# A two-layer streaming encoder on one core: grouping the up projections' high and low products, taking gate rows and two modulation folds from rounded halves, and moving the score mask from TensorE to VectorE

## The chip, the cores and the metric

The kernel runs on one core of one Trainium2 chip. The metric is the device time of one execution in microseconds (us), the median of several runs. The engines are called as the profile calls them: PE (TensorE's matmuls), PEld (its weight loads), DVE (VectorE), ACT (ScalarE), POOL (GpSimd) and SP (SyncE, which issues nearly all transfers).

## What is computed

Two layers with 256 positions, width 2048 and batch 1. Each layer first derives six modulation vectors from the conditioning vector `c`, then runs a mixer over four head groups and a gated feed-forward network:

```
mod = (silu(c) @ w_mod[l] + b_mod[l]).reshape(bn, 6, d)
h = layer_norm(x) * (1.0 + scale_m) + shift_m
proj = h @ w_in[l]                       # 2048 -> 4288, split among four groups
...
y = jnp.concatenate([y_a, y_b, y_c, y_d], axis=-1) @ w_out[l]
x = layer_norm(ALPHA * x + (1.0 + gate_m) * y, post_mix_g[l], post_mix_b[l])
h = layer_norm(x) * (1.0 + scale_f) + shift_f
y = conv_ffn(h, w_up[l], w_conv[l], b_conv[l], w_down[l])   # 2048 -> 2 x 5632 -> 2048
x = layer_norm(ALPHA * x + (1.0 + gate_f) * y, post_ffn_g[l], post_ffn_b[l])
```

Group B is an attention with four heads: within a block of 128 queries the first 64 may not see the last 64 keys (the mask is by chunks of 64). Everything is float32.

## The kernel before, in words

**Products from halves.** A float32 product costs PE two matmul records with the full operands. Where the kernel can, it instead splits a float32 operand into a rounded high half of type float32r and a low half (the rest), and sums three products: high x high, high x low and low x high. For the weights ACT writes the high half (`act.copy`, line 403) and DVE the low one (`tensor_tensor` subtract, line 404); for activations `split` (lines 418 to 421) does the same. The high and low weight tiles, `whi` and `wlo`, each hold 1024 columns and come from the pool `splitp` with four buffers for each name. The raw weights lie in four buffers of 8 KB per partition (`rawp`), which the modulation's weights (`wmod`) and the weights of the projections (`wraw`) share.

**One unit.** `stream` (lines 347 to 355) is the basic step. It issues the load and the split of the next unit's weights, then the products of the unit before (`flush`), and then `pump` advances the modulation stream by as many steps as the stage's rate in `RATES` allows. So a unit's weights are prepared while PE works on the unit before it. The framework's scheduler then orders each engine's instructions; an engine executes its own in that order, and waits where a result is not there yet.

**Up projections.** `group2` (lines 474 to 497) computes 512 channels of the up projection for all 256 positions, in four units of four 128-row weight tiles. It keeps four PSUM accumulators of 128 channels by 512 columns: columns 0 to 255 collect the products with the high half of the activations and columns 256 to 511 those with the low half. For each weight tile and each accumulator it issues one matmul with the high weights and 512 columns (line 491) and right behind it one with the low weights and 256 columns (line 492). There are 40 such groups: 9 for gates (`g_c`) and 10 for values (`v_c`) in layer 0, and 10 and 11 in layer 1. The down projection (`out_proj`, accumulators `d`) and the output projection (`o`) use 512 columns throughout; the mixer's `group` uses 256 columns throughout.

**Modulation.** `mod_stream` (lines 265 to 310) loads `w_mod` row tile by row tile and DVE accumulates it, scaled by `c`, into `macc`, [128 x 2048] (`mod_step`, line 211). What is left is the sum over the 128 partitions. For shifts and scales `mod_cols` (lines 190 to 204) makes columns: one float32 matmul for each 128 columns of `macc`, with `macc` as the weights and a column of ones as the moving operand. For gates `gate_rows` (lines 244 to 252) makes a row in all partitions: four float32 matmuls with a [128 x 128] tile of ones as weights and 512 columns of `macc` moving. `settle` (lines 258 to 263) calls one or the other, two steps into the next vector at the latest or when the result is needed.

**Attention.** `mix_b` (lines 870 to 1036) computes scores for four heads into `ps_sc`. For each head and query block there are two score products (lines 986 and 987) and a third matmul with one row of weights (line 988, `ind_row` and `neg_row`, both rows of the constant `cst`) that adds -1e30 where the mask forbids. DVE then takes the row maxima (line 991), ACT the exponentials, DVE the scaling, PE the transposes. The scheduler places products of the mixer's next group C (`C_c`) between these steps on PE. In layer 0 group C uses unsplit float32 weights (`wexact`, line 379), which lie in the same `whi` and `wlo` buffers as the halves.

**Start.** `ones` is set by POOL (lines 100 and 101); ACT computes silu of `c` (line 118), whose result the first modulation step needs.

Of the kernel before, what the change touches and what calls it, by code (L numbers as in the profile page):

```python
# [7 lines left out]
F32 = mybir.dt.float32  # L8
# [46 lines left out]
def encoder_kernel(ctx: ExitStack, tc: tile.TileContext, A: dict, consts: bass.AP, out: bass.AP):  # L55
# [44 lines left out]
    ones = keep.tile([P, P], F32, name="ones")  # L100
    pool.memset(ones, 1.0)
# [6 lines left out]
    ind_row = cst[64:65, 256:384]  # L108
    neg_row = cst[64:65, 384:448]
# [95 lines left out]

    def mod_step(acc, w, kt, first):
        col = cact[:, kt : kt + 1]
        if first:
            i = dve.tensor_scalar(out=acc, in0=w, scalar1=col, scalar2=None, op0=ALU.mult)
# [264 lines left out]
    def group2(w, c0, name, then, bg=0, spare=0):  # L474
# [5 lines left out]
        def products(item, u):  # L480
# [248 lines left out]
    def mixers(l, w_in, Y, hF=None, between=None):  # L729
# [140 lines left out]
        def mix_b(cps, _):  # L870
# [106 lines left out]
            for blk in range(2):  # L977
                nkey = P * (blk + 1)
                per = 512 // nkey
                for g in range(4 // per):  # L980
                    ps = ms_tile("ps_sc")
                    for i in range(per):
# [8 lines left out]
                    dve.tensor_reduce(out=sm[:, 0:per], in_=p3, axis=AX.X, op=ALU.max)  # L991
# [409 lines left out]
def _constants():  # L1401
# [18 lines left out]
    c[64, 256:320] = 1.0  # L1420
    c[64, 384:448] = NEG
# [32 lines left out]
```

## Time and profile before

| | |
|---|---|
| median of 3 runs | 2338.86 us (2335.3 to 2343.4) |
| the profiled execution's own time | 2342.81 us |
| its span in the profile | 2341.0 us |
| mean granted clock of PE | 0.986 |
| instructions on DVE, ACT, POOL | 2241, 1429, 59 |
| transferred | 605.19 MB, mean 259 GB/s |

The layer 0 mixer runs to about 334 us, its output projection to 438, its up projections to 974, its down projection to 1224; layer 1's mixer ends at 1476, its output projection at 1569, its up projections at 2085, its down projection at 2329. In the profile each matmul of the float32 kind shows as two records. The busy time of a matmul is modelled from its start to the end of its pipeline, so neighbours overlap; the distance from one start to the next is what it costs PE.

### The profile page before, as it was taken

The page shows a single profiled execution, that of the slowest core. Times are in us where ns is not written, and L with a number is a line of the kernel's source. Part 1 is how long each engine was busy: PE and PEld are TensorE (multiplying, and loading weights), DVE is VectorE, ACT ScalarE, POOL GpSimd, SP SyncE. Part 2 cuts the span into 40 slices and gives each one's busy share as a digit, 9 for nine tenths or more (in the row PEclk, how much of TensorE's full clock was granted, in tenths as well). Part 3 has the DMA queues.
Part 4 walks back from the last instruction along what each step waited for, and adds up shares of the span by engine and source line. Part 5 has one row for each costly group of instructions (what it writes and reads, how often), then busy time and mean ns, then how long its engine had stood idle before and what let it go on. Part 6 is the DMA issues. An engine that isn't in the chain of part 4 may idle for free. (4 is left out here: it accounts for less than half of the span.)

```text
span 2341.0 us, 31348 instructions
## 1 busy us (share of the span) xinstructions
PE 2273.2 (97%) x12407; PEld 1940.7 (83%) x12407; DVE 1784.2 (76%) x2241; ACT 1012.0 (43%) x1429; POOL 36.0 (2%) x59
## 2 busy tenths in 40 slices
PE   6899999999999999999999999989999999999997
PEld 4688886698888888888879999869888888888786
DVE  6868987778888788889975798886777755665676
ACT  2221141245445444544544434435454454454553
POOL 2000000000000000000000000000000000000000
PEclk9999999999999999999999999999999999999999
DMA  9999889588888798898865576774767655555554
GB/s 338 367 318 333 283 274 383 202 304 288 311 311 302 280 333 314 279 351 306 313 212 173 173 242 211 271 274 165 254 229 262 224 180 194 184 185 194 180 197 144
DMA packets 228731, 605.19 MB, mean 259 GB/s; under 512 B 14676, under 2 KB 27204, under 8 KB 210916
## 3 DMA queue, kind: packets, MB, share of 16 engines
q1 hardware_dynamic: 227800, 602.30, 73.7%
q8 instruction: 97, 1.59, 0.3%
q0 software_dynamic: 784, 0.90, 0.1%
q14 instruction: 50, 0.41, 0.1%
HBM read 601.05 MB, written 2.10 MB: 258 GB/s over the span
## 5 line engine op out<-in xcount | busy, mean ns | idle before, releaser
L404 DVE TENSOR_TENSOR wlo<-wraw,whi 128x1024 fp32r<-128x1024 f32 (+1 forms) x622 | 748.0, 1215 | 352.2 <-ACT whi L403 344.6
L403 ACT CAST whi<-wraw 128x1024 fp32r<-128x1024 f32 (+1 forms) x622 | 645.8, 1045 | 759.9 <-PE g_c L83 224.3
L83 PE MATMUL v_c<-hT,whi 128*128 128x512 f32 (+1 forms) x1456 | 499.3, 391 | 0.0
L83 PE MATMUL g_c<-hT,whi 128*128 128x512 f32 (+1 forms) x1344 | 452.4, 387 | 0.0
L83 PE MATMUL v_c<-hT,wlo 128*128 128x256 f32 x1400 | 395.2, 282 | 0.0
L83 PE MATMUL d<-whi,a 128*128 128x512 f32 x1344 | 389.4, 391 | 0.0
L211 DVE SCALAR_TENSOR_TENSOR macc<-wmod,cact,macc 128x2048 f32<-128x2048 f32 (+2 forms) x180 | 358.4, 1991 | 37.6 <-DMA wmod<-in_w_mod_dram 36.4
L83 PE MATMUL g_c<-hT,wlo 128*128 128x256 f32 x1280 | 359.5, 281 | 0.0
L83 PEld LDWEIGHTS v_c<-hT,whi 128*128 128x128 f32 x1456 | 271.6, 189 | 62.8 <-ACT whi L403 0.2
L83 PEld LDWEIGHTS d<-whi,a 128*128 128x128 f32 x1344 | 253.7, 189 | 53.2 <-issue 0.5
L83 PEld LDWEIGHTS g_c<-hT,whi 128*128 128x128 f32 x1344 | 248.3, 188 | 56.0
L83 PEld LDWEIGHTS v_c<-hT,wlo 128*128 128x128 f32 x1400 | 266.3, 190 | 0.4 <-DVE wlo L404 0.2
L83 PEld LDWEIGHTS g_c<-hT,wlo 128*128 128x128 f32 x1280 | 242.0, 189 | 0.0
L83 PE MATMUL d<-wlo,a 128*128 128x512 f32 x672 | 234.8, 392 | 0.7 <-DVE wlo L404 0.7
L83 PEld LDWEIGHTS d<-wlo,a 128*128 128x128 f32 x672 | 126.9, 189 | 27.9 <-DVE wlo L404 1.2
L420 ACT CAST a<-g 128x512 fp32r<-128x512 f32 x132 | 81.4, 617 | 63.1 <-PE d L83 62.1
L83 PE MATMUL o<-whi,a 128*128 128x512 f32 x352 | 99.8, 391 | 0.2 <-ACT whi L403 0.2
L756 DVE SCALAR_TENSOR_TENSOR convD<-gluD,pm,convD 128x255 f32<-128x255 f32 (+26 forms) x240 | 98.8, 459 | 0.5
L421 DVE TENSOR_TENSOR a<-g,a 128x512 fp32r<-128x512 f32 x132 | 88.7, 685 | 10.4 <-ACT a L420 10.3
L83 PE MATMUL D_c<-hT,whi 128*128 128x256 f32 x432 | 84.2, 296 | 2.7 <-ACT hT L420 2.0
L1210 DVE SCALAR_TENSOR_TENSOR u<-g,pf,u 128x254 f32<-128x254 f32 (+1 forms) x176 | 74.3, 477 | 10.7 <-ACT u L86 10.7
L211 DVE SCALAR_TENSOR_TENSOR qacc<-wmod,cact,qacc 128x1024 f32<-128x1024 f32 (+1 forms) x75 | 80.3, 1070 | 2.6 <-DMA wmod<-in_w_mod_dram 0.5
(297 smaller groups left out, 2514.2 us busy)
## 6 DMA issues: line engine op xcount, KB each, us to landing
wraw<-in_ffn_w_up_dram SPq DMA_DIRECT2D x168, 1024.0 KB, 5.7
wmod<-in_w_mod_dram SPq DMA_DIRECT2D x136, 1024.0 KB, 6.1
wraw<-in_ffn_w_down_dram SPq DMA_DIRECT2D x88, 1024.0 KB, 5.3
wmod<-in_w_mod_dram SPq DMA_DIRECT2D x64, 512.0 KB, 9.0
wraw<-in_w_in_dram SPq DMA_DIRECT2D x30, 1024.0 KB, 5.5
wexact<-in_w_in_dram SPq DMA_DIRECT2D x52, 512.0 KB, 7.3
wmod<-in_w_mod_dram SPq DMA_DIRECT2D x32, 768.0 KB, 6.3
wraw<-in_w_out_dram SPq DMA_DIRECT2D x24, 1024.0 KB, 7.1
```

The lines of the kernel that those rows point to most:

```text
L83: pe.matmul(o, lhsT, rhs, start=start, stop=stop, skip_group_check=True)
L211: i = dve.scalar_tensor_tensor(out=acc, in0=w, scalar=col, in1=acc, op0=ALU.mult, op1=ALU.add)
L403: act.copy(hi[:, :m], r)
L404: i = dve.tensor_tensor(out=lo[:, :m], in0=r, in1=hi[:, :m].bitcast(F32), op=ALU.subtract)
L420: act.copy(hi, src)
L421: dve.tensor_tensor(out=lo, in0=src, in1=hi.bitcast(F32), op=ALU.subtract)
L756: dve.scalar_tensor_tensor(out=yd[:, j, 30 - k :], in0=glu[:, j, : S - 30 + k], scalar=CW(k, j), in1=yd[:, j, 30 - k :], op0=ALU.mult, op1 ...
L1210: dve.scalar_tensor_tensor(out=u[:, sh:], in0=x[:, : S - sh], scalar=col(k, j), in1=u[:, sh:], op0=ALU.mult, op1=ALU.add)
```

## The change

There are four edits.

1. `group2`: for each pair of accumulators all high products of the unit's four weight tiles come first (eight matmuls of 512 columns), then all low ones (eight of 256 columns).
2. `gate_rows`: `macc` is split into float32r halves by ACT and DVE (new function `halves`, with its tiles in the `whi` and `wlo` buffers of `splitp`), and for each 512 columns two float32r matmuls with float32r ones as weights replace one float32 matmul.
3. `mod_rows` (new) replaces `mod_cols` for layer 1's feed-forward shift and scale only: the halves are summed by eight float32r matmuls of 512 columns whose weights are four columns of zeros and ones, so that row j of a [4 x 512] result is the j-th quarter; ACT copies it, four PE transposes turn it to columns, and DVE adds the bias.
4. The mask: the sixteen one-row matmuls go, and before each row maximum DVE adds -1e30 to 64 partitions of the scores in PSUM.

Besides, `ones` is now part of a float32r tile `onesR`, which POOL fills in pieces in a temporary and ACT copies.

```diff
+    flat = tmp_tile("flat")
+    pool.memset(flat[:, 0:P], 1.0)
+    pool.memset(flat[:, P : P + 16], 0.0)
+    for j in range(4):
+        pool.memset(flat[:, P + 5 * j : P + 5 * j + 1], 1.0)
+    onesR = keep.tile([P, P + 16], F32R, name="onesR")
+    act.copy(onesR, flat[:, : P + 16])
+    ones = onesR[:, 0:P].bitcast(F32)
...
+    def halves(acc, c0):
+        hi = splitp.tile([P, 1024], F32R, tag="whi", name="mhi")
+        lo = splitp.tile([P, 1024], F32R, tag="wlo", name="mlo")
+        split((hi, lo), acc[:, c0 : c0 + 1024])
+        return [(hi[:, i * 512 : (i + 1) * 512], lo[:, i * 512 : (i + 1) * 512]) for i in range(2)]
+
+    def mod_rows(l, m, acc):
+        ps = ms_tile("ps_row")
+        for j, pair in enumerate(halves(acc, 0) + halves(acc, 1024)):
+            for n, part in enumerate(pair):
+                mm(ps[0:4, :], onesR[:, P + 4 * j : P + 4 * j + 4], part, j + n == 0, j + n == 4)
+        row = tmp_tile("mrow")
+        act.copy(row[0:4, :], ps[0:4, :])
+        ps = ms_tile("ps_mod")
+        for i in range(4):
+            pe.transpose(ps[:, 4 * i : 4 * i + 4], row[0:4, i * P : (i + 1) * P], ident[0:4, 0:4])
+        cols = keep.tile([P, KT], F32, name=f"mod_{l}_{m}")
+        done = dve.scalar_tensor_tensor(
...
     def gate_rows(l, m, acc):
-        for q in range(4):
-            c = slice(q * 512, (q + 1) * 512)
-            ps = ms_tile("ps_gate")
-            mm(ps, ones, acc[:, c], True, True)
-            ident_act(g[:, c], ps, 1.0, ones[:, 0:1])
+        for h in range(2):
+            for i, (hi, lo) in enumerate(halves(acc, h * 1024)):
+                c0 = h * 1024 + i * 512
+                ps = ms_tile("ps_gate")
+                mm(ps, onesR[:, 0:P], hi, True, False)
+                mm(ps, onesR[:, 0:P], lo, False, True)
+                ident_act(g[:, c0 : c0 + 512], ps, 1.0, ones[:, 0:1])
...
+        elif (l, m) in ((1, SHIFT_F), (1, SCALE_F)):
+            mod_rows(l, m, acc)
...
             for part in (range(0, 2), range(2, 4)):
-                for k, (hi, lo) in enumerate(item):
-                    kt = u * nk + k
-                    both = box["h"][kt // 2][2][:, kt % 2, :, :]
-                    for i in part:
-                        o = box["c"][i]
-                        off = slice(i * P, (i + 1) * P)
-                        mm(o, hi[:, off], both.rearrange("p h t -> p (h t)"), kt == 0, False)
-                        mm(o[:, :S], lo[:, off], both[:, 0, :], False, kt == KT - 1)
+                for i in part:
+                    for k, (hi, _) in enumerate(item):
+                        kt = u * nk + k
+                        both = box["h"][kt // 2][2][:, kt % 2, :, :].rearrange("p h t -> p (h t)")
+                        mm(box["c"][i], hi[:, i * P : (i + 1) * P], both, kt == 0, False)
+                for i in part:
+                    for k, (_, lo) in enumerate(item):
+                        kt = u * nk + k
+                        high = box["h"][kt // 2][0][:, kt % 2, :]
+                        mm(box["c"][i][:, :S], lo[:, i * P : (i + 1) * P], high, False, kt == KT - 1)
...
-                        mm(o, rope[:, h // 2, qs], rope[:, 2 + h % 2, :nkey], False, False)
-                        mm(o[:, nkey - 64 :], ind_row, neg_row, False, True)
+                        mm(o, rope[:, h // 2, qs], rope[:, 2 + h % 2, :nkey], False, True)
                     sm = smallp.tile([P, 16], F32, tag="sm", name="sm", bufs=3)
                     p3 = ps.rearrange("p (i k) -> p i k", i=per)
+                    ahead = p3[0:64, :, nkey - 64 :]
+                    dve.tensor_scalar(out=ahead, in0=ahead, scalar1=NEG, scalar2=None, op0=ALU.add)
                     dve.tensor_reduce(out=sm[:, 0:per], in_=p3, axis=AX.X, op=ALU.max)
```

How the scheduler places this is read from the order of instructions on an engine. On PE, in layer 0's up projections, the first fold of layer 1 (the shift, `ps_mod`) stands between two groups before the change; `g_c` and `v_c` are the accumulators of the gate group that ends there and the value group that begins, `whi` and `wlo` the halves of the weights, `hT` the activations:

```order
L83 MATMUL g_c_5772<-hT,whi 128x512
L83 MATMUL g_c_5772<-hT,wlo 128x256
L83 MATMUL g_c_5773<-hT,whi 128x512
L83 MATMUL g_c_5773<-hT,wlo 128x256
L83 MATMUL ps_mod<-bcol_98,cst 128x16
L83 MATMUL ps_mod<-ones,macc 128x1 x16
L83 MATMUL v_c_5993<-hT,whi 128x512
L83 MATMUL v_c_5993<-hT,wlo 128x256
L83 MATMUL v_c_5994<-hT,whi 128x512
L83 MATMUL v_c_5994<-hT,wlo 128x256
```

The same place on PE after the change (`mhi` and `mlo` are the halves of `macc`, `ps_row` the [4 x 512] sum):

```order
L83 MATMUL g_c_5798<-hT,wlo 128x256 x4
L83 MATMUL g_c_5799<-hT,wlo 128x256 x4
L83 MATMUL ps_row<-mhi,onesR 4x512
L83 MATMUL v_c_6025<-hT,whi 128x512 x4
L83 MATMUL ps_row<-mlo,onesR 4x512
L83 MATMUL ps_row<-mhi,onesR 4x512
L83 MATMUL ps_row<-mlo,onesR 4x512
L83 MATMUL ps_row<-mhi,onesR 4x512
L83 MATMUL v_c_6026<-hT,whi 128x512 x4
L83 MATMUL v_c_6025<-hT,wlo 128x256
L83 MATMUL ps_row<-mlo,onesR 4x512
L83 MATMUL ps_row<-mhi,onesR 4x512
```

High and low products now stand in runs of four to one accumulator, and the fold's matmuls stand among the next group's products.

The second place is SP's order at the end of layer 0's mixer. `wexact` are group C's weights (a unit of C takes two), `wmod` those of the modulation, `wraw` those of the output projection that follows. Before:

```order
L381 DMA wexact<-in_w_in_dram 128x1024 x2
L299 DMA wmod<-in_w_mod_dram 128x1536 x2
L381 DMA wexact<-in_w_in_dram 128x1024 x2
L299 DMA wmod<-in_w_mod_dram 128x1536 x3
L381 DMA wexact<-in_w_in_dram 128x1024 x2
L389 DMA wraw<-in_w_out_dram 128x2x1024
L299 DMA wmod<-in_w_mod_dram 128x1536 x2
L389 DMA wraw<-in_w_out_dram 128x2x1024
```

After:

```order
L420 DMA wexact<-in_w_in_dram 128x1024 x2
L338 DMA wmod<-in_w_mod_dram 128x1536 x5
L428 DMA wraw<-in_w_out_dram 128x2x1024
L338 DMA wmod<-in_w_mod_dram 128x1536 x2
L428 DMA wraw<-in_w_out_dram 128x2x1024
L420 DMA wexact<-in_w_in_dram 128x1024 x4
L338 DMA wmod<-in_w_mod_dram 128x1536 x2
L428 DMA wraw<-in_w_out_dram 128x2x1024
```

The weights of C's last two units moved behind modulation tiles and the first two tiles of the output projection. In the program the halves of the first gate, which take buffers of the same names, now stand ahead of them.

On ACT the program's first instructions are now a table load, the copy to `onesR`, another table load and then silu of `c`; before there were one table load and silu.

More of the change, by code (lines that the diff above doesn't have):

```diff
@@ L99, in encoder_kernel @@
     sinT = cst[:, 768:1024]
-    ones = keep.tile([P, P], F32, name="ones")
-    pool.memset(ones, 1.0)
+    flat = tmp_tile("flat")
[6 more added lines that the diff above has]
+    ones = onesR[:, 0:P].bitcast(F32)
     mhalf = keep.tile([P, 4], F32, name="mhalf")
@@ L106, in power @@
         pool.tensor_tensor(out=o, in0=i, in1=mhalf[:, : i.shape[1]], op=ALU.pow)
-    ind_row = cst[64:65, 256:384]
-    neg_row = cst[64:65, 384:448]
     X = []
@@ L204, in mod_cols @@
             MOD_BY[(l, m, k0 + j)] = done.ins.name
+    def halves(acc, c0):
[15 more added lines that the diff above has]
+        done = dve.scalar_tensor_tensor(
+            out=cols.rearrange("p (i j) -> p i j", i=4),
+            in0=ps[:, 0:KT].rearrange("p (i j) -> p i j", i=4),
+            scalar=0.0 if m == SHIFT_F else 1.0,
+            in1=bcol[l][:, m * KT : (m + 1) * KT].rearrange("p (j i) -> p i j", i=4),
+            op0=ALU.add,
+            op1=ALU.add,
+        )
+        for k in range(KT):
+            at = 4 * (k % 4) + k // 4
+            MOD[(l, m, k)] = cols[:, at : at + 1]
+            MOD_BY[(l, m, k)] = done.ins.name
     def mod_step(acc, w, kt, first):
```

2 lines of the change are left out of this document (removed).

## The prediction

> **What bounds the kernel now.** I read the page first, for the busy shares and the clock over the span.
>
> ```profile
> PE 2273.2 (97%) x12407; PEld 1940.7 (83%) x12407; DVE 1784.2 (76%) x2241; ACT 1012.0 (43%) x1429; POOL 36.0 (2%) x59
> PE   6899999999999999999999999989999999999997
> DMA  9999889588888798898865576774767655555554
> ```
>
> PE works throughout; the transfers are dense only in layer 0, the first half. Then I read the chain that ended last, and the waits.
>
> ```profile
> by line: PE g_c L83 11.0%; PE v_c L83 10.6%; PE d L83 9.4%; DMA wraw<-in_ffn_w_down_dram 0.5%; DVE x L658 0.2%; PE ps_xT L533 0.2%; DVE x L655 0.2%; PE ps_gate L83 0.2%; issue 0.1%; DVE wlo L404 0.1%; DVE st_o1q L664 0.1%; ACT whi L403 0.1%
> ...
> 1583.12 0.44 PE ps_xT L533 x4
> ...
> 1610.75 22.61 PE v_c L83 x128
> ...
> 2085.62 119.75 PE d L83 x528
> ```
>
> ```profile
> DVE wlo L404 <- ACT whi L403: 344.6, 269, 4.4
> ...
> ACT whi L403 <- PE g_c L83: 224.3, 138, 3.5
> ```
>
> The chain is PE without a break, one group of 128 matmuls every 22.61 us. ACT waits for PE to release a weight buffer, not the reverse, so the feeders are ahead. The windows of an up stretch in each layer say by how much:
>
> ```profile
> 540.00:660.00 120.00, 120.00 (x682) 104.02 (x681) 102.45 (x108) 57.63 (x79) 0.00 (x0) 1.00 0.87 307
> 1700.00:2080.00 380.00, 380.00 (x2153) 329.54 (x2152) 247.17 (x318) 193.66 (x279) 0.00 (x0) 1.00 0.62 209
> ```
>
> DVE is busy 85% of the time in layer 0 and 65% in layer 1. What shortens PE's stream therefore shortens the kernel, with less reserve in layer 0.
>
> **Grouping the up products.** A pair (512 columns high, 256 low) costs 22.61/64 = 353.3 ns in the chain. Runs of 512 columns alone, in the down projection above, cost 119.75/528 = 226.8 ns each. For 256 columns alone I take the mixer's group C in the timeline:
>
> ```profile
> 1401.57 0.40 PE L83 MATMUL C_c<-hT,whi 128*128 128x256 f32 x2
> ...
> 1405.53 0.40 PE L83 MATMUL C_c<-hT,whi 128*128 128x256 f32 x2
> ```
>
> Between these starts lie 33 matmuls of 256 columns, 3.96/33 = 120 ns each. Two pure runs thus cost 226.8 + 120 = 346.8 ns a pair, 6.5 less than alternating. That alternation does not always pay this shows in one stretch, where it ran at the pure rate. From the first row of a group to that of the next:
>
> ```profile
> 833.24 0.39 PE L83 MATMUL g_c<-hT,whi 128*128 128x512 f32 x1
> ...
> 855.43 0.39 PE L83 MATMUL v_c<-hT,whi 128*128 128x512 f32 x1
> ```
>
> That is 22.19/64 = 346.7 ns. The pairs are counted in the groups by form:
>
> ```profile
> L83 PE MATMUL v_c<-hT,whi 128*128 128x512 f32 x1344 | 478.8, 400 | 0.0
> L83 PE MATMUL g_c<-hT,whi 128*128 128x512 f32 x1216 | 429.2, 397 | 0.0
> ```
>
> Of 2560 pairs five groups (320, from 833 to 944 us) ran fast already; 2240 x 6.6 ns = 14.8 us are to be had. A switch from high to low and back is left once in eight pairs, which keeps between 0 and 1.9 us of that. I take -13.9 us.
>
> The page "TensorE: Matmul & The Clock Gate" of the Trainium skill gives, under "Back-to-back issue gap", N/2.4 + 2.5 ns from start to start of an isolated matmul, thus 325 ns for a pair in either order, and no gain from grouping; the rows show 353 and 347, so here the trace differs from it.
>
> **The two folds.** Before, each is a run of small matmuls between two groups. The timeline at both places, and the windows of the clock behind them (the column before the DMA share):
>
> ```profile
> 805.69 0.29 PE L83 MATMUL ps_mod<-bcol,cst 128*128 128x16 f32 x2
> ...
> 809.40 0.48 PE L83 MATMUL v_c<-hT,whi 128*128 128x512 f32 x1
> ```
>
> ```profile
> 944.17 0.29 PE L83 MATMUL ps_mod<-bcol,cst 128*128 128x16 f32 x2
> 944.31 5.01 PE L83 MATMUL ps_mod<-ones,macc 128*128 128x1 f32 x32
> 949.19 0.77 PE L83 MATMUL v_c<-hT,whi 128*128 128x512 f32 x1
> ```
>
> ```profile
> 810.00:813.00 3.00, 3.00 (x11) 2.51 (x11) 2.72 (x5) 2.79 (x6) 0.00 (x0) 0.50 0.00 0
> 947.00:953.00 6.00, 6.00 (x23) 5.42 (x24) 2.85 (x4) 3.32 (x7) 0.00 (x0) 0.50 0.30 126
> ```
>
> The folds take 3.71 and 5.02 us, and during or after them the granted clock is 0.50, which costs the next group half of 3.0 us and half of 3.8 (949.19 to 953): 1.5 and 1.9. Together 12.1 us. After: eight matmuls of 512 columns at 227 ns and four transposes (0.44 us in the chain above for larger ones), 2.3 us each, 4.5 in all, spread among full-size products. That is -7.6 us if the clock stays up, -4.2 if it still drops; I take -7, near the first, because no drop is seen among full-size products here.
>
> **The gates.** The first of four:
>
> ```profile
> 306.01 3.78 PE L83 MATMUL ps_gate<-macc,ones 128*128 128x512 f32 x8
> 309.63 0.59 PE L83 MATMUL C_c<-hF,wexact 128*128 128x256 f32 x2
> ```
>
> It holds PE for 3.62 us; after, eight products of 227 ns, 1.82. Four times 1.8, less a little since part of the 3.62 is waiting: -6.8 us.
>
> **What the halves cost.** Six steps (four gates, two folds) copy and subtract twice each. From the page:
>
> ```profile
> L404 DVE TENSOR_TENSOR wlo<-wraw,whi 128x1024 fp32r<-128x1024 f32 (+1 forms) x622 | 748.0, 1215 | 352.2 <-ACT whi L403 344.6
> L403 ACT CAST whi<-wraw 128x1024 fp32r<-128x1024 f32 (+1 forms) x622 | 645.8, 1045 | 759.9 <-PE g_c L83 224.3 <-PE v_c L83 172.9 <-PE d L83 134.8
> ```
>
> That is 12 x 1.05 us on ACT and 12 x 1.22 on DVE. The work itself fits into their idle time. But each step takes two of the four buffers of `whi` and `wlo`, so the unit after next can be split only when PE releases the unit before it, not a unit earlier. Its first copy (1.05) and subtraction (1.22) begin about a quarter of a unit (1.4 us) before PE needs them; its second ones begin at the unit's end. In the up stage the low halves are wanted only after eight high products (1.8 us), so about 0.5 us is left uncovered; in the output and down projections, which are not regrouped, about 0.7 to 1. Behind these subtractions DVE holds the modulation steps, which nothing waits for at once. I take +4 us for the six, between 0 and 10.
>
> In layer 0's mixer the order on SP moves the weights of C's last two units back until C's fourth-last and third-last units have released their buffers.
>
> ```profile
> wexact<-in_w_in_dram SPq DMA_DIRECT2D x52, 512.0 KB, 7.3
> ```
>
> ```profile
> 312.65 10.96 PE L83 MATMUL C_c<-hF,wexact 128*128 128x256 f32 x50
> ```
>
> They land 7.3 us after issue; a C unit of 16 products is 32 records, at 10.96 us for 50 about 7 us. Issue at the end of one unit thus meets the start of the next but one narrowly: +1 us, between 0 and 3.
>
> **The mask.** On PE its cost is from its start to the next product's:
>
> ```profile
> 1395.47 0.43 PE L83 MATMUL ps_sc<-cst 1*128 1x64 f32 x2
> 1395.84 0.49 PE L83 MATMUL ps_sc<-kn,qn 128*128 128x128 f32 x2
> ```
>
> 0.37 us, sixteen times: -5.9 us. On DVE six additions in PSUM come in. The trace has none; the nearest rows are the maximum over the same tile and a four-element operation:
>
> ```profile
> 1399.25 0.68 DVE L991 TENSOR_REDUCE sm<-ps_sc 128x4 f32<-128x512 f32 x1
> ...
> 1400.22 0.22 DVE L992 TENSOR_SCALAR sm<-sm,rr 128x4 f32<-128x4 f32 x1
> ```
>
> Between 0.22 and 0.68, about 0.4 for half the size, 2.4 in all on the score chain. PE has products of C to do meanwhile, and the scheduler has put the transposes further behind; I charge +1 (0 to 4).
>
> **The start.** ACT has a copy and a second table load ahead of silu, and POOL five more small fills.
>
> ```profile
> 0.73 1.28 ACT L118 ACT_TABLE_LOAD   x1 [0.73 <-PEq L1433]
> 3.02 0.31 ACT L118 ACTIVATE crow<-crow 16x128 f32<-16x128 f32 x1 [1.01 <-DMA crow<-in_c_dram]
> ```
>
> ```profile
> 14.33 0.49 DVE L209 TENSOR_SCALAR qacc<-wmod,cact 128x512 f32<-128x512 f32 x1 [0.29 <-DMA wmod<-in_w_mod_dram]
> ```
>
> Silu moves from 3.0 to about 4.5 us; its first user starts at 14.33. Cost nothing, as long as that transfer ends last.
>
> **The sum.** -13.9 - 7 - 6.8 + 4 + 1 - 5.9 + 1 = -27.6 us. The profiled execution took 2342.81 us (1.8 of it outside the span), which gives 2315.2; I forecast **2315 us**. It is the slowest but one of what was shown: the median of the runs is 2338.86, 4 us less, against which the forecast is 24 us or 1.0% faster. I do not carry those 4 us over: runs of before can differ in how many groups fall into the fast alternation, and grouped runs have no such choice.
>
> **The rivals.**
>
> - *The order of high and low does not matter.* What costs 6.6 ns a pair is then not the switch but something that runs of eight have too. For it: the stretch at 833 us switches and pays nothing. Against it: pure runs never show more than 227 and 120 ns. The first term falls away: 2315 + 14 = 2329 us. The Trainium skill's formula above would have it so.
> - *The halves break the feeding.* Each of the six steps leaves PE idle for the copy and subtraction of a whole unit, twice 1.05 + 1.22 = 4.5 us instead of 0.7: 6 x 3.8 = 23 us more, 2338 us, no change. For it: DVE at 85% in layer 0. Against it: the scheduler has put the low products of the gates behind the next group's high ones.
> - *Slower: the low tiles are held longer.* With all low products last, a unit's first `wlo` buffer is read until 0.24 us before the unit's end instead of 1.4; the next subtraction in that buffer, and with it the raw buffer and the next transfer, come 1.17 us later. It decides once DVE has no idle time left in a unit. In layer 0's 76 units (19 groups of 4), half of them late by 1.17 us give +44: 2359 us. Against it: the 15% idle there, and that low products are wanted 1.6 us later too.
>
> **How the numbers follow.** The forecast gets 0.76, the first rival 0.1, the second 0.1, the third 0.04. The forecast's own bounds: every gain full and no stall is 14.8 + 7.6 + 7.2 + 5.9 = 35.5, 2307 us; stalls of 10, C late by 3, the mask's 4 and the clock still dropping (2.8) give 2315 + 14 = 2329, where the first rival lies as well. So 2306 to 2329, with the second and third rival left out. About 0.3% (7 us) is what a measurement can tell from no change: faster by more, under 2331.8, is forecast and first rival and part of the second, 0.9; the same 0.06; slower 0.04.
>
> **What would show it.** In the profile of the changed kernel a group of 128 up matmuls should take 22.2 us throughout; the clock should be 1.00 around the two folds; the gates' eight products should each be 227 ns apart; 16 one-row matmuls should be gone. PE waiting for `wlo` after a gate or fold, or for `wexact` before the end of C, shows the charges. Groups still at 22.6 us, or PE waiting for `wlo` in every layer 0 unit, make the prediction wrong.

## The result and the profile after

| | before | after |
|---|---|---|
| median, same chips | 2337.55 us (2330.69 to 2345.99, 10 runs) | 2329.73 us (2323.61 to 2334.77, 10 runs) |
| the profiled execution | 2342.81 us | 2328.31 us |

The ratio is 0.9962, with a 95% interval of 0.9945 to 0.9978: faster by 7.8 us or 0.4%. The forecast was 2315 us with a range of 2306 to 2329, so the time lies 0.7 us above the range and the gain is about a third of what was forecast against the median.

The page of the kernel after shows PE busy 97% as before, of a shorter span:

```profile
PE 2255.9 (97%) x12331; PEld 1936.7 (83%) x12331; DVE 1792.9 (77%) x2261; ACT 1011.3 (43%) x1443; POOL 37.6 (2%) x64
```

The chain that ended last (start, us, what), at the place where before had 22.61 us for a group of 128:

```profile
1625.38 22.35 PE g_c L83 x128
...
2072.31 119.72 PE d L83 x528
```

A group takes 22.35 us, 349.2 ns a pair, not 22.2. The timeline inside a group, one run of eight high and eight low products after another:

```profile
1700.64 2.00 PE L83 MATMUL v_c<-hT,whi 128*128 128x512 f32 x8
1702.48 1.11 PE L83 MATMUL v_c<-hT,wlo 128*128 128x256 f32 x8
1703.43 2.00 PE L83 MATMUL v_c<-hT,whi 128*128 128x512 f32 x8
```

From high run to high run it is 2.79 us. Eight pairs at the pure rates of the prediction (226.8 and 120 ns) would be 2.774, so a change from low to high and back costs about 20 ns, and it falls within the high run: 1.84 us for eight is 230 ns each, while the low run has 0.95, 119 each.

The folds stand as the order had them, and cost what was forecast. The timeline from the start of one of them to the next group, and the clock (before the DMA share) over both groups:

```profile
795.96 0.40 PE L83 MATMUL ps_row<-mhi,onesR 128*4 128x512 f32 x1
...
820.87 1.32 PE L83 MATMUL g_c<-hT,whi 128*128 128x512 f32 x5
```

```profile
796.00:821.00 25.00, 24.99 (x143) 1.00 0.74 263
932.00:958.00 26.00, 26.00 (x150) 1.00 0.79 273
```

Fold and group took 833.24 - 805.69 = 27.55 us before and take 24.91 now; the other fold with its group went from 29.56 to 24.71. Together that is -7.5 us, and the clock stays at 1.00.

New are waits of PE for the low halves. The groups by form, the column behind the second bar being PE's idle time before these products, first of before, then of after. The rows hold both layers' down projections: before's 0.7 us lies at the end of layer 1's, and of after's 4.1 us, 2.9 lie in layer 0's.

```profile
L83 PE MATMUL d<-wlo,a 128*128 128x512 f32 x672 | 234.8, 392 | 0.7 <-DVE wlo L404 0.7
L83 PE MATMUL o<-wlo,a 128*128 128x512 f32 x176 | 58.3, 390 | 1.4 <-DVE wlo L404 1.4
```

```profile
L83 PE MATMUL d<-wlo,a 128*128 128x512 f32 x672 | 235.1, 392 | 4.1 <-DVE wlo L443 4.0
L83 PE MATMUL o<-wlo,a 128*128 128x512 f32 x176 | 59.1, 395 | 5.5 <-DVE wlo L443 5.5
```

By stage, from the first product of one to the first of the next in the timelines of the two profiled executions:

| stage | before | after | change |
|---|---|---|---|
| start and first mixer groups | 194.45 | 193.25 | -1.2 |
| layer 0: B, C, to the output projection | 139.66 | 135.22 | -4.4 |
| layer 0: output projection and norm | 189.75 | 190.55 | +0.8 |
| layer 0: up projections | 449.86 | 438.29 | -11.6 |
| layer 0: down projection | 252.19 | 259.56 | +7.4 |
| layer 1: mixer before C | 143.22 | 146.25 | +3.0 |
| layer 1: C | 78.73 | 74.35 | -4.4 |
| layer 1: E, output projection, norm | 162.62 | 165.32 | +2.7 |
| layer 1: up projections | 474.95 | 469.37 | -5.6 |
| layer 1: down projection to the end | 255.57 | 254.36 | -1.2 |

Together -14.5 us, as the two profiled times say. Six stages gave 28.4 us and four took 13.9 of it back. The experiments ask two things: why grouping gave so little, and what made the new waits.

### The profile page after: what moved, and what is told of

It is laid out like the page before. It is cut to its first block, busy times and chain, and to the rows that moved or that the text cites. A ratio compares the mean times of both kernels' runs of the same rounds, so it can differ in the third digit from the quotient of the medians.

```text
span 2326.5 us, 31205 instructions
## 1 busy us (share of the span) xinstructions
PE 2255.9 (97%) x12331; PEld 1936.7 (83%) x12331; DVE 1792.9 (77%) x2261; ACT 1011.3 (43%) x1443; POOL 37.6 (2%) x64
## 5 line engine op out<-in xcount | busy, mean ns | idle before, releaser
L442 ACT CAST whi<-wraw 128x1024 fp32r<-128x1024 f32 (+1 forms) x622 | 633.0, 1044 | 735.9 <-PE g_c L83 208.6
L83 PE MATMUL v_c<-hT,whi 128*128 128x512 f32 (+1 forms) x1456 | 358.7, 384 | 0.0
L83 PE MATMUL g_c<-hT,whi 128*128 128x512 f32 (+1 forms) x1344 | 327.7, 382 | 0.0
L83 PEld LDWEIGHTS v_c<-hT,whi 128*128 128x128 f32 x1456 | 259.3, 189 | 43.5
L83 PEld LDWEIGHTS v_c<-hT,wlo 128*128 128x128 f32 x1400 | 194.5, 190 | 13.7
L83 PE MATMUL v_c<-hT,wlo 128*128 128x256 f32 x1400 | 203.9, 282 | 0.0
L83 PEld LDWEIGHTS g_c<-hT,wlo 128*128 128x128 f32 x1280 | 178.2, 190 | 11.8
L83 PE MATMUL g_c<-hT,wlo 128*128 128x256 f32 x1280 | 187.7, 282 | 0.0
L797 DVE SCALAR_TENSOR_TENSOR convD<-gluD,pm,convD 128x255 f32<-128x255 f32 (+25 forms) x240 | 99.2, 459 | 0.6
L83 PEld LDWEIGHTS o<-whi,a 128*128 128x128 f32 x352 | 66.8, 190 | 14.1 <-ACT whi L442 0.3
```

The lines of the kernel that those rows point to most:

```text
L83: pe.matmul(o, lhsT, rhs, start=start, stop=stop, skip_group_check=True)
L442: act.copy(hi[:, :m], r)
L797: dve.scalar_tensor_tensor(out=yd[:, j, 30 - k :], in0=glu[:, j, : S - 30 + k], scalar=CW(k, j), in1=yd[:, j, 30 - k :], op0=ALU.mult, op1 ...
```

## The experiments

Each kernel was timed beside the kernel before on the same chip; the first four share 35 runs of it (median 2339.95 us, 2327.62 to 2348.75), the next four 29 (2341.91 us, 2329.52 to 2352.12).

**Grouping alone** (the kernel before with the edit of `group2` only):

```diff
...
-                        mm(o, hi[:, off], both.rearrange("p h t -> p (h t)"), kt == 0, False)
-                        mm(o[:, :S], lo[:, off], both[:, 0, :], False, kt == KT - 1)
+                for i in part:
+                    for k, (hi, _) in enumerate(item):
...
+                for i in part:
+                    for k, (_, lo) in enumerate(item):
...
```

> The kernel before with the grouping of the up products alone. Theory S (a switch from low to high costs about 20 ns in grouped runs, read from the changed kernel's profile, where 64 pairs with 8 switches take 22.35 us): a group of 128 up matmuls takes 22.35 us instead of 22.61, 35 to 40 groups gain 0.26 each, the time falls by 8 to 9 us (ratio about 0.9963). Theory P (the prediction: only 0 to 6.6 ns stay per eight pairs): groups at 22.2 us, 13 to 15 us less (0.994), and then what is missing in the changed kernel was lost in other stages.

Measured: 2338.11 us (2332.84 to 2342.75, 12 runs), ratio 0.9995 (0.9978 to 1.0013). Every group takes 22.35 us in the chain, as in the kernel after, and yet the median does not move: the interval holds -5 to +3 us. Both theories miss it, S with 8 to 9 us less and P with 13 to 15. If all 40 groups of the kernel before took 22.61 us in every execution, 40 x 0.26 = 10.4 us would have come off; so the 22.61 us of the first profile cannot be what every group takes in every execution.

**Everything but grouping** (the kernel after with the old loop in `group2`):

```diff
-                for i in part:
-                    for k, (hi, _) in enumerate(item):
...
+                        mm(o, hi[:, off], both.rearrange("p h t -> p (h t)"), kt == 0, False)
+                        mm(o[:, :S], lo[:, off], both[:, 0, :], False, kt == KT - 1)
```

> The changed kernel with the old alternation of high and low in the up products; gates, folds and mask changed. Theory S: the other three edits together give only what is left of 8.9 us, 0 to 5 us (ratio 0.998 to 1.000), because the gate of layer 1's output projection stalls PE and the clock drops elsewhere. Theory P: the other three give their 14 to 17 us (ratio 0.993 to 0.994).

Measured: 2327.48 us (2318.23 to 2336.42, 12 runs), ratio 0.9952 (0.9931 to 0.9972). The other three edits give the whole gain as far as the intervals can tell: 11 us (7 to 16), more than theory S's 0 to 5 and less than P's 14 to 17, which the interval still touches. In its profile the alternating groups of layer 0 run at 346.7 ns a pair up to the first fold and at 353.3 behind it, and those of layer 1 at 353.3.

**Runs of sixteen** (the kernel after, with all four accumulators in one part):

```diff
-            for part in (range(0, 2), range(2, 4)):
+            for part in (range(0, 4),):
```

> The changed kernel with runs twice as long: in each unit all sixteen high products of the four accumulators, then all sixteen low ones. Theory S: half of the switches go, 160 x 20 ns = 3.2 us less than the changed kernel, a group at 22.27 us. Rival (the excess belongs to the high products themselves, not to the switch): a group stays at 22.35 us and the time at that of the changed kernel. If low products then come too late in the unit for the release of buffers, PE would wait for wlo and the time would rise.

Measured: 2326.52 us (2321.66 to 2331.58, 12 runs), ratio 0.9948 (0.9931 to 0.9965). Its chain:

```profile
1620.26 22.27 PE g_c L83 x128
```

Four changes in a group instead of eight make it 0.08 us shorter: 20 ns for a change again. Forty groups make 3.2 us, which is the difference of the two medians against the kernel after, though these two were not timed beside each other.

**Everything but the gates** (the kernel after with the old body of `gate_rows`):

```diff
-        for h in range(2):
-            for i, (hi, lo) in enumerate(halves(acc, h * 1024)):
...
+                mm(ps, ones, acc[:, c], True, True)
...
```

> The changed kernel with the old gate rows (four float32 matmuls). Theory G (the halves of a gate delay the low weights behind them on DVE): the wait of 5.5 us for wlo behind layer 1's first gate falls to about 1.4, the four gates cost PE 4 x 1.8 = 7 us more, together +2 to +4 us against the changed kernel. Rival (the halves cost next to nothing, the stall is due to the order of the residual step alone): the wait stays, +7 us. If halves cost more than they bring, the time falls.

Measured: 2330.26 us (2323.24 to 2333.67, 12 runs), ratio 0.9956 (0.9937 to 0.9974), no different from the kernel after, so the time does not tell theory G's +2 to +4 us from nothing. The waits do: without the gates' halves the one in layer 1's output projection is back at its old size, as G has it. Those in layer 0's down projection stay (2.37 and 0.61 us); the 1.05 us that the kernel after waits in layer 1's down projection, behind its second gate, goes:

```profile
L83 PE MATMUL d<-wlo,a 128*128 128x512 f32 x672 | 235.2, 393 | 3.3 <-DVE wlo L441 3.3
L83 PE MATMUL o<-wlo,a 128*128 128x512 f32 x176 | 58.3, 390 | 1.4 <-DVE wlo L441 1.4
```

**The mask alone:**

```diff
-                        mm(o, rope[:, h // 2, qs], rope[:, 2 + h % 2, :nkey], False, False)
-                        mm(o[:, nkey - 64 :], ind_row, neg_row, False, True)
+                        mm(o, rope[:, h // 2, qs], rope[:, 2 + h % 2, :nkey], False, True)
...
+                    dve.tensor_scalar(out=ahead, in0=ahead, scalar1=NEG, scalar2=None, op0=ALU.add)
```

> The kernel before with the mask edit alone. Theory M: the sixteen one-row matmuls go (5.9 us of PE) and DVE's six additions are hidden, so layer 1's stage from group C's first product to E's (78.7 us before) comes to about 74.3 as it did with all edits; with the same in layer 0 that is -8 to -9 us: 2331 us. Prediction on record: -4.9 us, 2335. Theory M also says: up products alternate here, and in each stretch between two drops of the granted clock all their groups run at one of two speeds, 22.2 or 22.6 us from first to first; and PE does not wait for wlo over 1 us in layer 0's down projection. Rival: the mask's change of order is what brings that wait (2.7 us), then it is here.

Measured: 2334.39 us (2327.1 to 2343.61, 12 runs), ratio 0.9979 (0.9957 to 1.0001). Between -10 and 0 us holds theory M's -8 as well as the -4.9 on record. The stage of C in layer 1 is more exact: 75.17 us, -3.6, less than M's -4.4 and more than the -2.5 or so that the record had per layer. The rival on the wait falls: PE has no wait for `wlo` in the down projections at all (0.0 in the row that had 0.7 before).

**The two folds alone** (the kernel before with `onesR`, `halves`, `mod_rows` and the branch that calls it):

```diff
...
+        elif (l, m) in ((1, SHIFT_F), (1, SCALE_F)):
+            mod_rows(l, m, acc)
```

> The kernel before with the two folds from halves alone. Theory M: the two folds give back 7.5 us in layer 0's up projections and the clock drops there are gone; but the fold of the next shift, which stood right behind the first half of the down projection's residual (554 of its products ahead of it) and gave PE 3.7 us of work while DVE does the residual, now stands before it (504), so PE waits there for wlo 2 to 3 us that it did not wait before. Net -4 to -5 us: 2335. Rival: that wait belongs to the halves' buffers or to another edit; then layer 0's down projection takes 252.2 us as before and the gain is 7.5: 2332.

Measured: 2333.4 us (2322.2 to 2344.33, 12 runs), ratio 0.9962 (0.994 to 0.9984), -8.9 us with -4 to -14 in the interval, so the sum of M (-4 to -5) is at its edge. The place of the wait is as M said: layer 0's down projection takes 258.90 us instead of 252.19, and its timeline shows the wait of 2.35 us:

```profile
1100.31 0.50 PE L83 MATMUL d<-wlo,a 128*128 128x512 f32 x1 [2.35 <-DVE wlo L443]
```

Its up groups in layer 1 alternate at the other rate, which no other profile of an alternating kernel shows there:

```profile
1632.18 22.19 PE g_c L83 x128
```

**The gates alone** (as the folds, with the new `gate_rows` and without the `elif`):

```diff
...
+                mm(ps, onesR[:, 0:P], hi, True, False)
+                mm(ps, onesR[:, 0:P], lo, False, True)
...
```

> The kernel before with the gate rows from halves alone. Theory M: layer 0's two gates and layer 1's second give 1.8 to 2 us of PE each, layer 1's first gives as much but PE then waits 5.9 us for wlo instead of 1.8 because DVE does the gate's two subtractions and all eight residual operations first; the stage of layer 1's output projection takes 101.4 us instead of 99.3, the end of the second down projection has a wlo wait of 1.4 us. Net -2 to -4 us: 2337. Layer 0's down projection stays at 252 us. Rival (prediction on record): four times 1.7 less, with 0.7 of wait each: -4 us, spread evenly, and no wait above 1 us.

Measured: 2335.67 us (2328.74 to 2346.16, 12 runs), ratio 0.9979 (0.9959 to 0.9999). The time can't tell M from its rival, the stages can: layer 1's output projection takes 101.55 us instead of 99.34 with a wait of 5.53, not 0.7, its second down projection 255.50 instead of 255.57; layer 0's B and C take 137.87 instead of 139.66, and its down projection 252.30 as before.

```profile
1525.12 0.80 PE L83 MATMUL o<-wlo,a 128*128 128x512 f32 x1 [5.53 <-DVE wlo L443]
```

**Runs of sixteen, one old gate, and the cover put back.** Three things differ from the kernel after: the loop of the runs of sixteen, layer 1's first gate by the old four float32 matmuls, and the fold of layer 1's mixer shift held behind the 540th product of layer 0's down projection (`after_d` lists these):

```diff
...
+        i = mm(ps[:, 0:n], ident, bcol[l][:, m * KT + k0 : m * KT + k0 + n], True, False)
+        if (l, m) == (1, SHIFT_M):
+            tc.add_manual_dep(i.ins, after_d[540].ins.name, order_dep, reason="the fold covers the residual")
...
+        if (l, m) == (1, GATE_M):
...
+                mm(ps, ones, acc[:, c], True, True)
...
```

> The changed kernel with three things altered: high and low products of the up projections in runs of sixteen; layer 1's first gate row from float32 as before; and the fold of layer 1's mixer shift held behind the 540th product of layer 0's down projection, so that it stands beside DVE's residual again. Theory M: against the run with runs of sixteen alone (2326.5), layer 1's output projection falls from 101.5 to 99.1 and layer 0's down projection from 255.9 to about 253.4, with no wait for wlo over 1 us there: 2322 us. Rival: the waits only move to the next wlo, and the time stays at 2326.

Measured: 2318.31 us (2314.14 to 2322.59, 6 runs), ratio 0.9899 (0.9874 to 0.9924), the fastest of all kernels here. Layer 0's down projection takes 252.32 us and layer 1's output projection 99.18, both as before the change; with runs of sixteen alone they took 255.93 and 101.49. PE has no wait for `wlo` left in layer 0's down projection, and the 1.1 us below lies in layer 1's, where the kernel after has it too. So the rival, that the waits only move on, falls:

```profile
L83 PE MATMUL d<-wlo,a 128*128 128x512 f32 x672 | 234.4, 391 | 1.1 <-DVE wlo L454 1.1
L83 PE MATMUL o<-wlo,a 128*128 128x512 f32 x176 | 58.7, 393 | 1.4 <-DVE wlo L454 1.4
```

**The kernel before, profiled twice more.** No edit.

> The kernel before, unchanged, for a second profile of the same program. Theory L: the speed of alternating high and low products, 346.7 or 353.3 ns a pair, is drawn anew in an execution wherever another kind of matmul has come between; then at least one of the three long stretches (540 to 805 us, 833 to 944, 1610 to 2085; 353.3, 346.7 and 353.3 in the first profile) has the other speed in this profile or in the next one. With a chance of one half for each, all six the same as before has a chance of 1 in 64. Rival: the order of the program decides it; then all three stretches run as in the first profile.

> The kernel before once more, third profile. Theory L: as for the second profile; layer 1's up stage takes 474.95 us or, if it draws the other speed, 466.0. Rival: 474.95 and the same pattern of 353.3, 346.7, 353.3 ns.

Measured: 2348.03 and 2346.17 us, one run each; a third run of it on this chip took 2346.51. In the second profile the groups between gate and first fold, and those between the two folds (starts of the first products of successive groups):

```profile
718.77 0.39 PE L83 MATMUL v_c<-hT,whi 128*128 128x512 f32 x1
...
740.96 0.39 PE L83 MATMUL g_c<-hT,whi 128*128 128x512 f32 x1
...
835.45 0.40 PE L83 MATMUL g_c<-hT,whi 128*128 128x512 f32 x1
...
858.06 0.40 PE L83 MATMUL v_c<-hT,whi 128*128 128x512 f32 x1
```

They take 22.19 and 22.61 us. In the first profile the same two stretches had 22.62 (its rows below) and 22.19 us (the rows in the prediction): both have changed sides, in one and the same program.

```profile
692.61 0.40 PE L83 MATMUL g_c<-hT,whi 128*128 128x512 f32 x1
...
715.23 0.40 PE L83 MATMUL v_c<-hT,whi 128*128 128x512 f32 x1
```

In the third profile both stretches have 22.19. So the rival falls, and the fixed order does not decide alone. Theory L's even chance for each stretch is not borne out, though: the first five groups of layer 0 and all of layer 1 ran at 22.61 in all three. Among the other alternating kernels (everything but grouping, mask, folds, gates alone) layer 0's first stretch ran at 22.2 in all four, and layer 1's at 22.61 in three. The kernels also ran on different chips. What picks the rate, and whether the program or the chip shifts the odds, stays open.

**Runs of four** (the kernel after, with an accumulator's low products right behind its four high ones):

```diff
...
-                for i in part:
                     for k, (_, lo) in enumerate(item):
...
```

> The changed kernel with the up products in runs of four high and four low to one accumulator: 16 changes from low to high in a group of 128 instead of 8. Theory S: each change costs 20 ns whatever the length of the run, so the group's first-to-last distance is 22.23 + 0.16 = 22.39 us, 351.7 ns a pair in every group, and layer 1's up stage 469.4 + 21 x 0.16 = 472.7 us. Rival: the cost of a change shrinks with the run, as alternation with 0 or 6.6 ns a pair suggests; then the group takes at most 22.3 us, or 22.1 where it is free.

Measured: 2333.55 us in one run, beside 2346.51 for the kernel before. The chain has 22.45 us a group:

```profile
1628.40 22.45 PE g_c L83 x128
```

Theory S said 0.16 us more than the kernel after; it is 0.10. A change costs (22.45 - 22.19)/16 = 16 ns here, and 20 in runs of eight and sixteen; its rival (22.3 at most) is off by more. The cost does shrink with the run, to 16 ns at four and to 0 or 6.6 at one, but slowly.

## Why the prediction was wrong, step by step

**Grouping (-13.9): the step that failed.** Two sizes in it were wrong: the cost of a change, and the number of pairs that pay for alternation. First, "a switch from high to low and back is left once in eight pairs, which keeps between 0 and 1.9 us": I took the most that a change can cost from alternation, 6.6 ns. A change behind a run of eight costs 20 ns, three times that bound, so a grouped pair takes 349.2 ns instead of 346.8. Against the first profile of before that leaves 2240 pairs x 4.1 = 9.2 us of gain and 320 x 2.5 = 0.8 of loss, -8.4. Second, "2240 pairs" are the pairs of one execution. I saw that executions can differ in this and did not put it into the sum or the range. Alternation runs at 346.7 or 353.3 ns, stretch by stretch; if all 2560 pairs had the lower rate, grouping at 349.2 would cost 2560 x 2.5 = 6.4 us, and if all had the higher, give 10.5. Measured is 0.9995, with -5 to +3 us in the interval. The spread speaks for this: in the four grouped kernels with ten or twelve runs (after, grouping alone, runs of sixteen, everything but gates) the times lie within 10 to 11 us, in the four alternating ones of the experiments within 17 to 22. Grouped alone, runs lay between 2333 and 2343 us; 6 less at the low end and 10 more at the high one gives 2327 to 2353, and the kernel before showed 2327.6 to 2352.1. By this account grouping took away a spread and hardly a cost. It is argued, not shown: the three profiled executions of the kernel before (2342.8, 2348.0 and 2346.2 us) are all slower than its median, and by the rates of their groups each would have gained some 6 to 8 us from grouping, more than the interval's 5. No execution of it under the median has a profile, and only the folds alone showed the lower rate in layer 1. So it is shown that grouping did not pay what was forecast and that a change costs 20 ns; why the median did not move at all stays open.

The first rival, that the order does not matter, gave 2329 us and so the right time, but by chance: in the profiles the order does matter (349.2 ns against 346.7 or 353.3), only the medians of the two orders cannot be told apart, and that rival's sum also holds the other terms at sizes that they did not have. The Trainium skill, in "TensorE: Matmul & The Clock Gate", section "Back-to-back issue gap", gives an isolated gap of N/2.4 + 2.5 ns, which makes an estimate of 325 for the pair, whatever the order. No arrangement here came under 346.7: alternation gave 346.7 or 353.3, runs of sixteen 347.9 (22.27 us a group), of eight 349.2, of four 350.8. The trace disagrees with it in size and in that the order counts.

**The two folds (-7): right,** -7.5, with no drop of the clock.

**The gates (-6.8) and the halves (+4): right in the parts that PE alone sets, wrong where DVE does.** Layer 0's two gates gave 1.8 us in the mixer and about 2 in the up projections, with no wait behind them; the eight products stand 230 to 240 ns apart where they follow each other, and 420 or so where the one ahead comes behind a float32 product:

```profile
301.52 0.58 PE L83 MATMUL ps_gate<-mhi,onesR 128*128 128x512 f32 x1
301.94 0.40 PE L83 MATMUL ps_gate<-mlo,onesR 128*128 128x512 f32 x1
302.18 0.40 PE L83 MATMUL ps_gate<-mhi,onesR 128*128 128x512 f32 x1
```

Layer 1's first gate is another matter. The order on DVE and on PE in the timeline of after:

```profile
1513.26 2.36 DVE L460 TENSOR_TENSOR mlo<-macc,mhi 128x1024 fp32r<-128x1024 f32 x2
1516.38 1.29 DVE L675 TENSOR_TENSOR yg<-o,gate 128x512 f32<-128x512 f32 x2 [0.76 <-ACT gate L86]
...
1523.57 4.61 DVE L443 TENSOR_TENSOR wlo<-wraw,whi 128x1024 fp32r<-128x1024 f32 x4
```

```profile
1518.46 0.84 PE L83 MATMUL o<-whi,a 128*128 128x512 f32 x3
1524.83 0.79 PE L83 MATMUL o<-wlo,a 128*128 128x512 f32 x1 [5.53 <-DVE wlo L443]
```

DVE does the gate's two subtractions (2.4 us), then the residual of four tiles (7.2 us), and only then the low halves that PE needs. Before, the subtractions were not there and PE's gate took longer beside the residual; PE waited 1.41:

```profile
1529.88 1.22 DVE L404 TENSOR_TENSOR wlo<-wraw,whi 128x1024 fp32r<-128x1024 f32 x1
```

```profile
1531.16 0.50 PE L83 MATMUL o<-wlo,a 128*128 128x512 f32 x1 [1.41 <-DVE wlo L404]
```

Both can be counted from the start of DVE's modulation step ahead (1521.17 us before, 1511.99 after). DVE comes to the low half 2.9 us later than before: 11.58 us behind that step instead of 8.71, by the two subtractions and by the residual's last operation, which stood behind the low half before. PE comes to its wait (1531.16 - 1.41 before, 1524.83 - 5.53 after) 1.3 us earlier: 7.31 us behind the start of that step instead of 8.58. Together that is 4.1, and 5.53 - 1.41 is 4.12. At this place DVE was already the later one, so saving PE's time there is worth nothing and each DVE operation counts in full. The prediction looked for the cost in the buffers, about 0.7 us a step, and not in what stands on DVE between the halves and the next `wlo`. In all, the gates with their waits came to some -1.5 us instead of -4.1 (-6.8 and four sixths of the +4 for the halves).

**Not in the prediction: a fold that was cover.** The largest loss, 7.4 us in layer 0's down projection, has no term in the sum. Before, the fold of layer 1's mixer shift stood behind the first 554 products, where DVE does the residual before it makes the next low half. The timeline of before on PE and on DVE:

```profile
1099.46 3.71 PE L83 MATMUL ps_mod<-ones,macc 128*128 128x1 f32 x32
...
1103.25 0.58 PE L83 MATMUL d<-wlo,a 128*128 128x512 f32 x1
```

```profile
1099.24 2.33 DVE L211 SCALAR_TENSOR_TENSOR macc<-wmod,cact,macc 128x2048 f32<-128x2048 f32 x1
1101.49 2.35 DVE L404 TENSOR_TENSOR wlo<-wraw,whi 128x1024 fp32r<-128x1024 f32 x2
```

PE folds for 3.7 us while DVE finishes, and the low half is there when it is done. After the change the scheduler puts this fold, whose code the change does not touch, behind 504 products, ahead of the residual, and DVE's same work stands bare (after, PE and DVE):

```profile
1073.62 2.54 PE L83 MATMUL ps_mod<-onesR,macc 128*128 128x1 f32 x15
...
1089.50 0.84 PE L83 MATMUL d<-whi,a 128*128 128x512 f32 x3
1092.69 0.50 PE L83 MATMUL d<-wlo,a 128*128 128x512 f32 x1 [2.35 <-DVE wlo L443]
```

```profile
1089.17 2.33 DVE L246 SCALAR_TENSOR_TENSOR macc<-wmod,cact,macc 128x2048 f32<-128x2048 f32 x1
1091.42 2.35 DVE L443 TENSOR_TENSOR wlo<-wraw,whi 128x1024 fp32r<-128x1024 f32 x2
```

With a second wait of 0.56 us that is 2.9 us. The clock takes 3.4 more: around the two folds of this stage it was 0.91 and 0.89 of full over 18 and 16 us before, thus 3.4 us lost, and is 0.81 and 0.79 after, 6.8 lost.

```profile
1097.00:1115.00 18.00, 18.00 (x92) 0.91 0.68 253
1162.00:1178.00 16.00, 16.00 (x82) 0.89 0.43 141
```

```profile
1067.00:1085.00 18.00, 18.00 (x85) 0.81 0.65 232
1152.00:1168.00 16.00, 16.00 (x74) 0.79 0.41 137
```

The remaining 1.1 us I could not assign. The two folds alone bring the wait; grouping, gates or mask alone do not; and with the fold put back it is gone, while the two other edits of that kernel, each in a run without the fold's, leave it (3.30 us with runs of sixteen, 2.37 and 0.61 with all gates as before). So the place of the fold is the cause of the wait. The clock's share is another matter. In the seven profiles with the fold behind 554 products (the three of before, grouping, mask, gates alone, and the fold put back) the drops cost 3.4 us each time and the stage takes 252.2 to 253.5 us. In the six with the fold moved ahead they cost 3.4 us in two, 5.1 in three and 6.8 in the kernel after, and the stage takes 255.9 to 259.6. Against 252.2 us the moved fold thus costs 3.7 us at the least, and the 7.4 of the profiled execution are the most that was seen; putting it back gave 3.6 us against the run of sixteen alone (255.93 to 252.32). That the fold moved stands in the order on PE of the two programs; the prediction reads that order at the two edited places alone.

**C's last weights in layer 0 (+1): nothing.** PE waits for no `wexact` between 236 and 336 us.

**The mask (-5.9 + 1): the gain was there and the charge was not.** In layer 1 the distance from C's first to last product with high weights (the last two numbers ahead of the forms), before and after:

```profile
L83 PE MATMUL C_c<-hT,whi x256: 278/283/469, 1369.1 to 1447.6; 128*128 128x256 f32 x128
```

```profile
L83 PE MATMUL C_c<-hT,whi x256: 278/283/469, 1363.1 to 1437.2; 128*128 128x256 f32 x128
L1032 DVE TENSOR_SCALAR ps_sc<-ps_sc x3: 282/283/418, 1393.0 to 1412.4; 64x128 f32<-64x128 f32 x2, 64x256 f32<-64x256 f32 x1
```

It falls from 78.5 to 74.1 us, more than eight times 0.37. The additions take 0.28 and 0.42 us, as estimated, hidden beside C's products. Layer 0's mixer as a whole gave 4.4, of which 1.8 is the gate's; these two are differences of single profiles, and the same stage of the kernel before took 142.76 and 141.23 us in its other two profiles, not 139.66, so here they are rough.

**The start (0): right** as far as it can be told; the stage came 1.2 us earlier, with fewer drops of the clock.

**The sum.** Against the profiled execution: grouping -8.4 instead of -13.9; folds -7.5 instead of -7; gates with their waits about -1.5 instead of -4.1; the halves of the folds, charged 1.3, cost 7.4 in this execution through the fold they displaced; the mask about -7 instead of -4.9. That is -17; layer 1's mixer outside C took 4.3 us longer, of which 3.0 are drops of the clock that the third profile of before has as well (below), and the rest, the start above all, gives -1.8. Against the median, grouping is -1 with -5 to +3, and everything else 0.9952, -11. That the time still came within 1 us of the range is partly luck: the sum starts from an execution 5.3 us above the median of before; from 2337.55 the same terms would have given 2310 us, 20 too few. The chances were wrong in the same place: I had weighed rivals for each step but none in which the first profile was not typical, although the prediction itself says that runs of before can differ in it.

## What to carry to other kernels

When one profile shows the same work at two rates, profile the unchanged kernel a second time before the difference is counted as a gain: here the larger term of the forecast was within what executions of one program differ by. Before an edit shortens or moves a step on the engine that is never idle, ask what the step covers, and compare the whole order of that engine before and after: a fold of 3.7 us that no edit touched moved ahead of the work that it had covered. Three small corrections (longer runs, one gate as before, one fold put back) took the ratio from 0.9962 to 0.9899, more than the four edits had brought, though these two were not timed beside each other. Where the waiting engine already waits, as at layer 1's first gate, only what the other engine does counts.

## What the runs showed of the hardware

A pair of float32r products, 512 and 256 columns with a weight load each, runs at one of two rates when it alternates, 346.7 or 353.3 ns, constant over whole groups in these profiles and changing only where other matmuls or another stage come between. Longer runs have one rate that depends on their length (350.8, 349.2, 347.9 ns for four, eight, sixteen) and repeats in every group.

The clock's drops differ between executions of one program. The windows of the clock over 10 us at the start of layer 1's mixer and behind the wait for its first D products, in the first and then in the third profile of before:

```profile
1225.00:1235.00 10.00, 9.03 (x78) 1.00 0.95 325
1261.00:1271.00 10.00, 9.69 (x78) 1.00 0.50 147
```

```profile
1227.00:1237.00 10.00, 9.29 (x66) 0.83 0.97 329
1264.00:1274.00 10.00, 9.36 (x63) 0.83 0.44 141
```

That is 3.4 us at half clock at each place in one and none in the other, and some 1.5 us on the stage each time: the mixer before C takes 143.22 us in the first profile and 146.27 in the third. The profile of after had both drops (0.83 at each place) and 146.25 us, so the +3.0 in that mixer is no more than two executions of the kernel before differ by. The Trainium skill says in "TensorE: Matmul & The Clock Gate", section "The HAM clock gate (the "warmup" mystery)", that activity is judged in windows of some 3.4 us that run freely, so that where they fall differs from run to run; the trace agrees as far as it shows this, with drops of 3.4 and 6.8 us, and the same wait of 2.7 us ahead of the D products with and without one.
